# Moving operands 128 bytes further into their room: y's halves and the forms t1 and t3

## The chip, the cores and the metric

The kernel runs on one core of a Trainium2 chip. The metric is device time in microseconds (us) for one execution, taken as the median of the executions timed. The kernel before takes 1009.21 us, the median of three (1008.97, 1009.21 and 1009.24).

In the profile the engines are called PE (the matrix engine; PEld is its loading of stationary operands), DVE (the vector engine), ACT (the scalar engine), POOL and SP. ACT, DVE and POOL compute, and SP issues most of the transfers from device memory.

## The reference, cut to what matters

One block: a root-mean-square norm, one wide projection, two branches (a gated convolution and a state-space scan), a mixing product and a gated feed-forward. All of it is float32, with 512 tokens and a model width of 1024. The change touches an operand of two products: the gate-linear projection `u_glu` and the output product of the scan branch, `y @ out_w`.

```python
h = rms_norm(x, mix_pre_g[i])
proj = h @ w_in[i]
u_glu = proj[..., :OFF_Z]                 # val and gt of the gated convolution
...
val, gt = jnp.split(u_glu + glu_b, 2, axis=-1)
v = val * jax.nn.sigmoid(gt)
...
# scan branch
y = ssd_chunked(...)                      # [tokens, 2048]
y = y * jax.nn.silu(z)
yg = y.reshape(bsz, seqlen, N_GROUPS, D_INNER // N_GROUPS)
yg = yg * lax.rsqrt(jnp.mean(yg * yg, axis=-1, keepdims=True) + RMS_EPS)
y = yg.reshape(bsz, seqlen, D_INNER) * norm_g
ssm_out = y @ out_w                       # [512, 2048] @ [2048, 1024]
...
mixed = (g_conv * conv_out + g_ssm * ssm_out) @ w_out[i]
```

## The kernel before

**Split products.** PE multiplies in a rounded float32 format, so each float32 operand is kept as two halves, a high one and a low one, and each product is three matmuls into the same accumulator: high by high, high by low, low by high. `mm3` issues them (lines 426, 428 and 432). Each matmul has a stationary operand of 128 by 128, loaded first, and a moving operand that streams past it: 128 partitions by 512 columns (a whole row of tokens) or by 256 (half of it). In a row of the profile such as `pso<-yhl,whi` the accumulator stands before the arrow, then the moving operand, then the stationary one.

**The scan branch's output, `ssm_out`.** y comes in four pairs of groups, p = 0 to 3. For each pair the high and low halves of y lie in one tile, `yhl` (it is made again for every pair, always in the same room; its name in the trace drops the number). `s4` fills it: PE transposes y into an accumulator (`pyT`), ACT writes the high half (line 1051), DVE the low one (line 1052). `ssm_out` then makes 8 outputs `pso` per pair, each of 4 steps by 3 matmuls of 512 columns with `yhl` moving and the weights `whi` and `wlo` stationary: 4 x 8 x 4 x 3 = 384 matmuls. For p = 0, 1 and 2 they run in two runs of 48, for p = 3 in one of 96, broken in places by a few small matmuls of the scan.

**The gated projection's second half.** Units u = 0 to 3 use a scheme of seven half-size products in place of eight. Its moving operands are sums and differences of parts of h, each 256 columns wide: b11, b21 and b22 lie in `hhi` and `hlo`, and four forms t1 to t4 are made by `h_forms` (ACT on line 612 writes the high halves, DVE on line 613 the low ones). t1 and t3 share a tile in the room of `yhl` (which is free then), t4 and t2 a tile in the room called "so". The trace calls both tiles `h_t`. Each product is 4 steps by 3 matmuls. t2 is used in `glu_x` (stationary `whi_..S`, first half), t1 in `glu_v` (`whi_..s`, accumulator `pgv`), t3 in `glu_y` (`whi_..C`, accumulator `pgx`), b22 in `glu_w`, t4 in `glu_z`. So t1 and t3 move in 4 x 2 x 4 x 3 = 96 matmuls.

**Order.** The order of the instructions on every engine is written out in tables (`ORDER_ACT`, `ORDER_DVE`, `ORDER_PE`, and so on), which `in_written_order` enforces.

**Where the operands lie.** Tiles are laid out by pools with fixed places. In the built program the moving operands of these matmuls start, in bytes modulo 512, at the following places. Every step of an operand begins a multiple of 512 bytes after the last, so all steps share the place.

| moving operand | columns | place modulo 512 |
|---|---|---|
| `hhi`, `hlo` (whole rows: px, pB, pC, pgs, pgc) | 512 | 160 |
| `ehi`, `elo` (pg, pv in the first 40 us) | 512 | 160 |
| `yhl` (pso) | 512 | 32 |
| b11, b21, b22 in `hhi`, `hlo` (glu) | 256 | 160 |
| t1, t3 (glu) | 256 | 224 |
| t4, t2 (glu) | 256 | 352 |

The stationary operands of all these matmuls, `whi` and `wlo`, start at 160 modulo 512. `elo` lies in the same pool as `yhl`, `ehi` in the same room as t4 and t2. The room of `yhl` has 512 bytes more than y's halves fill, and the two offsets of the change (128 bytes, and 128 + 192) stay within them.

Of the kernel before, what the change touches and what calls it, by code (L numbers as in the profile page):

```python
# [11 lines left out]
F32R = mybir.dt.float32r  # L12
# [6 lines left out]
P = 128  # L19
T = 512  # L20
# [4 lines left out]
K2 = NK // 2  # L25
# [59 lines left out]
ADD_LO = (2, 3) + tuple(range(7, FF // P, 2))  # L85
GU_AHEAD = 5
MOV_AT = 192
S_AHEAD = 5

TAPS_GLU = 12  # L90
# [268 lines left out]
def block_kernel(ctx: ExitStack, tc: tile.TileContext, x, xT, x0, prm, hp, gp, wf, w, out):  # L359
# [87 lines left out]
    def col(name, i):  # L447
        o = PRM_OFF[name] + i
        return prm_t[:, o : o + 1]
# [25 lines left out]
    ssd = br.enter_context(tc.tile_pool(name="ssd", bufs=1))  # L475
# [12 lines left out]
    def aux_tile(name):  # L488
        return in_turn("aux", 2, 3, name)
# [107 lines left out]

    def h_forms():
        rooms = [p.tile([P, 8 * T + P], F32R, tag=tg, name=f"h_{n}") for p, tg, n in ((ssd, "yhl", "t13"), (sp, "so", "t42"))]
        both = [[r[:, MOV_AT // 4 + i * 4 * T : MOV_AT // 4 + (i + 1) * 4 * T].rearrange("p (n k t) -> p n k t", n=2, k=K2) for i in range(2)] for r in rooms]  # L600
        for f, two in zip(both, (("t1", "t3"), ("t4", "t2"))):
            for i, n in enumerate(two):
                HF[n] = [a[:, i] for a in f]
        for k in range(K2):
            (b11, b12), (b21, b22) = [(xk[q][:, :T2], xk[q][:, T2:T]) for q in (k, K2 + k)]
            dve.tensor_tensor(out=b11, in0=b11, in1=b12, op=ALU.subtract)
            dve.tensor_tensor(out=b12, in0=b22, in1=b12, op=ALU.subtract)
            dve.scalar_tensor_tensor(out=b22, in0=b22, scalar=-1.0, in1=b11, op0=ALU.mult, op1=ALU.subtract)
            dve.scalar_tensor_tensor(out=b21, in0=b22, scalar=-1.0, in1=b21, op0=ALU.mult, op1=ALU.subtract)
            for q, (hi, lo) in zip((k, K2 + k), both):  # L610
                t = xk[q].rearrange("p (n t) -> p n t", n=2)
                act.copy(hi[:, :, k], t)
                dve.tensor_tensor(out=lo[:, :, k], in0=t, in1=hi[:, :, k].bitcast(F32), op=ALU.subtract)
        for n, k0, c in (("b11", 0, slice(0, T2)), ("b21", K2, slice(0, T2)), ("b22", K2, slice(T2, T))):
            HF[n] = [a[:, k0 : k0 + K2, c] for a in (hhi, hlo)]
# [248 lines left out]
    proj_z0()  # L864
    time_steps()
    h_forms()
    for i, tg in enumerate(("xdt", "y")):
        n = seq["val", EARLY + 2] + i
# [171 lines left out]
    def s4(g):  # L1040
        s = st[g]
        yz = s["y"].rearrange("p c h d -> p c (h d)")
        if g % 2 == 0:
            yhl = ssd.tile([P, 8 * T + P], F32R, tag="yhl", name=f"yhl{g}")
            ys[g // 2] = [yhl[:, i * 4 * T : (i + 1) * 4 * T].rearrange("p (k t) -> p k t", k=4) for i in range(2)]
        yh, yl = ys[g // 2]
        for e in range(2):
            ps = aux_tile(f"pyT{g}_{e}")
            for c in range(NT):
                pe.transpose(ps[:, c * P : (c + 1) * P], yz[:, c, e * P : (e + 1) * P], ident)  # L1050
            act.activation(yh[:, 2 * (g % 2) + e, :], ps, AF.Copy, scale=col("norm_g", 2 * g + e))
            dve.scalar_tensor_tensor(
                out=yl[:, 2 * (g % 2) + e, :], in0=ps, scalar=col("norm_g", 2 * g + e),
                in1=yh[:, 2 * (g % 2) + e, :].bitcast(F32), op0=ALU.mult, op1=ALU.subtract,
            )
        del st[g]
# [18 lines left out]
    for g in range(G):  # L1075
# [5 lines left out]
        if g % 2 and g > 1:  # L1081
            s4(g - 2)
# [9 lines left out]
        if g % 2 == 0 and g > 1:  # L1092
            s4(g - 2)
# [35 lines left out]
    s1(G - 1)  # L1129
    gate("gs", 1, sg_tile("sgs1"))  # L1130
    s4(G - 2)
    s2(G - 1)
    gate("gs", 2, sg_tile("sgs2"))
# [12 lines left out]
    vp = mid.enter_context(tc.tile_pool(name="vT", bufs=1))  # L1146
    vp.tile([P, MOV_AT // 4], F32, name="vT_place")
    VF = {n: [vp.tile([P, K2, T2], F32R, name=f"v_{n}{p}") for p in "hl"] for n in ("t4", "b11", "b21", "t2", "t1", "t3", "b22")}
# [217 lines left out]
    mov, at = {}, [0]  # L1366

    def place_at(pool_, to):

        n = (to - at[0]) % 512  # L1370
        if n:
            pool_.tile([P, n // 4], F32, tag=f"place{at[0]}", name=f"place{at[0]}")
            at[0] += n

    place_at(h2p, MOV_AT)
    for n in MOV:
# [472 lines left out]
    for i, key in enumerate(STEPS):  # L1849
        while done_to < min(len(ahead), i + S_AHEAD + 1):  # L1850
            prep(ahead[done_to])
# [122 lines left out]
```

## Time and profile before

| what | value |
|---|---|
| median of the runs | 1009.21 us |
| the profiled execution's own time | 1009.96 us |
| its span, first to last instruction | 1008.2 us |
| granted PE clock over the span | 0.998 |
| PE busy | 1000.1 us (99%) |
| DVE busy | 875.3 us (87%) |
| ACT busy | 671.4 us (67%) |
| `pso` matmuls | 384 rows, 230 to 541 us |
| `pgv` and `pgx` matmuls with t1 or t3 | 96 rows, 70 to 101 us |

A row of a group of instructions gives line, engine, operation, tiles, shape and count, then after the bar the busy time in us, the mean duration of one in ns, and the idle time of the engine just before. Matmuls are pipelined: a 512-column matmul lasts some 390 ns from its start to its end, but the next one starts some 227 ns after it. What a matmul costs the engine is therefore read from the times at which rows start, in a view of the instructions in order of time, and not from its duration.

### The profile page before, as it was taken

What the parts mean: (1) busy time and instruction counts of PE and PEld (TensorE: products, weight loads), DVE (VectorE), ACT (ScalarE), POOL (GpSimd) and SP (SyncE); (2) the same over time, 40 slices, a digit from 0 to 9 for tenths busy, and PEclk for the clock granted to TensorE, in tenths of its full rate; (3) what the DMA queues carried; (4) which work ended last, traced back from release to release, by engine and by line L of the source; (5) the groups of instructions that cost most, each with busy time, mean ns of one, the idle gap of its engine ahead of it and who ended that gap; (6) DMA issues with size and microseconds to landing.
All of it is one profiled execution on the core that took longest, in us unless ns stands there. A gap on an engine that the chain in (4) does not pass through costs nothing.

```text
span 1008.2 us, 16310 instructions
## 1 busy us (share of the span) xinstructions
PE 1000.1 (99%) x6296; PEld 881.8 (87%) x6296; DVE 875.3 (87%) x1285; ACT 671.4 (67%) x1102; POOL 121.1 (12%) x145
## 2 busy tenths in 40 slices
PE   9999999999999999999999999999999999999997
PEld 7899889888888888888888889889999999998886
DVE  7899999838997999899996688889999897899974
ACT  8577789898667756854442585587666666667552
POOL 0210211110123022001110020011000000001001
PEclk9999999999999999999999999999999999999999
DMA  8755945646651684357453255646556455469622
GB/s 304 214 135 145 257 117 160 189 123 149 167 147 42 170 214 123 83 143 171 102 130 99 84 128 187 230 124 169 167 147 180 135 147 146 141 177 294 204 84 83
DMA packets 44557, 156.62 MB, mean 155 GB/s; under 512 B 5184, under 2 KB 6208, under 8 KB 43456
## 3 DMA queue, kind: packets, MB, share of 16 engines
q1 hardware_dynamic: 30672, 105.44, 31.3%
q0 software_dynamic: 11888, 44.57, 22.6%
q10 hardware_dynamic: 1920, 5.57, 1.6%
q8 instruction: 49, 0.80, 0.3%
q14 instruction: 28, 0.23, 0.1%
HBM read 151.31 MB, written 4.26 MB: 154 GB/s over the span
## 4 chain that ended last, share of the span: by engine, by line
PE 97%; DMA 1%; ACT 1%; DVE 0%; issue 0%; SPq 0%; POOL 0%; POOLq 0%; DVEq 0%; ACTq 0%
PE xy L432 4%; PE xy L426 4%; PE xy L428 4%; PE pso L426 3%; PE pz L428 3%; PE pz L432 3%; PE pz L426 3%; PE pso L432 3%; PE pso L428 3%; PE px L428 3%; PE px L426 3%; PE px L432 3%; PE yv L428 2%; PE yv L432 2%; PE yv L426 2%; PE yd L997 2%
## 5 line engine op out<-in xcount | busy, mean ns | idle before, releaser
L699 DVE SCALAR_TENSOR_TENSOR a<-v,prm_t,a 128x507 f32<-128x507 f32 (+20 forms) x240 | 171.5, 756 | 0.7
L391 ACT CAST whi<-raw 128x1024 fp32r<-128x1024 f32 x91 | 94.5, 1046 | 72.0 <-PE pso L428 27.4
L398 DVE TENSOR_TENSOR wlo<-raw,whi 128x1024 fp32r<-128x1024 f32 x54 | 65.6, 1218 | 32.2 <-ACT whi L391 32.2
L396 POOL DMA_DIRECT2D wlo<-in_w x37 | 32.9, 888 | 285.1 <-ACT wlo L395 83.4
L432 PE MATMUL pz<-whi,hlo 128*128 128x512 f32 (+2 forms) x160 | 56.1, 352 | 0.0
L428 PE MATMUL pz<-wlo,hhi 128*128 128x512 f32 (+2 forms) x160 | 55.8, 350 | 0.0
L426 PE MATMUL pz<-whi,hhi 128*128 128x512 f32 (+2 forms) x160 | 55.4, 352 | 0.0
L426 PE MATMUL pso<-yhl,whi 128*128 128x512 f32 x128 | 50.8, 399 | 0.0
L1407 ACT CAST whi_g<-raw 128x1024 fp32r<-128x1024 f32 x40 | 41.4, 1052 | 13.7 <-DVE raw L1438 7.5
L432 PE MATMUL pso<-yhl,wlo 128*128 128x512 f32 x128 | 50.4, 395 | 0.0
L426 PE MATMUL px<-hhi,whi 128*128 128x512 f32 x128 | 50.4, 393 | 0.0
L428 PE MATMUL pso<-yhl,whi 128*128 128x512 f32 x128 | 50.3, 395 | 0.0
L432 PE MATMUL px<-hhi,wlo 128*128 128x512 f32 x128 | 49.9, 389 | 0.0
L428 PE MATMUL px<-hlo,whi 128*128 128x512 f32 x128 | 49.8, 389 | 0.0
L1412 DVE TENSOR_TENSOR wlo_g<-raw,whi_g 128x1024 fp32r<-128x1024 f32 x34 | 41.2, 1220 | 3.4 <-ACT whi_g L1407 3.4
L682 ACT ACTIVATE L<-L,nacs 128x128 f32<-128x128 f32 x128 | 42.8, 392 | 1.3 <-POOL L L676 1.0
L890 DVE SCALAR_TENSOR_TENSOR x<-px,prm_t,x 128x511 f32<-128x511 f32 (+2 forms) x48 | 35.5, 743 | 6.2 <-ACT x L888 6.0
L395 ACT ACTIVATE wlo<-whi 128x1024 fp32r<-128x1024 f32 x37 | 39.1, 1058 | 0.4
L426 PEld LDWEIGHTS pz<-whi,hhi 128*128 128x128 f32 x160 | 30.2, 188 | 3.9
L428 PEld LDWEIGHTS pz<-wlo,hhi 128*128 128x128 f32 x160 | 30.2, 188 | 3.8
L432 PEld LDWEIGHTS pz<-whi,hlo 128*128 128x128 f32 x160 | 30.2, 188 | 3.8
L1407 ACT CAST chi_g<-raw 128x1024 fp32r<-128x1024 f32 x24 | 24.9, 1054 | 10.1 <-PE yv L428 3.4
(1046 smaller groups left out, 3618.1 us busy)
## 6 DMA issues: line engine op xcount, KB each, us to landing
raw<-in_w SPq DMA_DIRECT2D x182, 512.0 KB, 4.3
wlo<-in_w POOLq DMA_DIRECT2D x37, 512.0 KB, 5.8
L<-scr POOLq DMA_DIRECT2D x8, 1024.0 KB, 5.7
wlo_g<-in_w POOLq DMA_DIRECT2D x11, 512.0 KB, 5.8
sums<-in_w POOLq DMA_DIRECT2D x16, 256.0 KB, 4.5
clo_g<-in_w POOLq DMA_DIRECT2D x6, 512.0 KB, 5.7
pw_raws<-in_w SPq DMA_DIRECT2D x4, 512.0 KB, 6.2
xr<-in_x ACTq DMA_DIRECT2D x4, 512.0 KB, 4.2
```

The lines of the kernel that those rows point to most:

```text
L391: act.copy(hi[:, c], src)
L395: act.activation(lo[:, c], hi[:, c].bitcast(F32), AF.Copy, scale=-1.0)
L396: pool.dma_start(lo[:, c], w[n][:, c].bitcast(F32R), accum_op=ALU.add)
L398: dve.tensor_tensor(out=lo[:, c], in0=src, in1=hi[:, c].bitcast(F32), op=ALU.subtract)
L426: pe.matmul(ps, lh, rh, start=start, stop=False, skip_group_check=more)
L428: pe.matmul(ps, lh, rl, start=False, stop=False, skip_group_check=more)
L432: pe.matmul(ps, ll, rh, start=False, stop=stop, skip_group_check=more)
L682: act.activation(L[:, h, c, :], L[:, h, c, :], AF.Exp, bias=nacs[:, c, HG * g + h : HG * g + h + 1])
L699: return dve.scalar_tensor_tensor(out=va[j][:, d:], in0=vs[j][:, : T - d], scalar=col("dw_w", j * KC + KC - 1 - d), in1=va[j][:, d:], op0= ...
L890: dve.scalar_tensor_tensor(out=a[:, d:], in0=ps[:, : T - d], scalar=col("ssm_w", i * KS + KS - 1 - d), in1=a[:, d:], op0=ALU.mult, op1=ALU ...
L1407: act.copy(hi, src)
L1412: dve.tensor_tensor(out=lo, in0=src, in1=hi.bitcast(F32), op=ALU.subtract)
```

## The change

The tile `yhl` is viewed from 128 bytes into its room, so y's halves start at 160 modulo 512. The tile of t1 and t3, in the same room, is used from 128 + 192 bytes in, so these forms start at 352. The forms t4 and t2 stay where they are. No tile is moved or resized: every allocation of the built program has its address as before. The order of the instructions on all five engines is the same, row for row, and of the matmuls only the 384 with `yhl` and the 96 with t1 or t3 read from another address.

```diff
 MOV_AT = 192
+YHL_AT = 128
 S_AHEAD = 5
...
     def h_forms():
         rooms = [p.tile([P, 8 * T + P], F32R, tag=tg, name=f"h_{n}") for p, tg, n in ((ssd, "yhl", "t13"), (sp, "so", "t42"))]
-        both = [[r[:, MOV_AT // 4 + i * 4 * T : MOV_AT // 4 + (i + 1) * 4 * T].rearrange("p (n k t) -> p n k t", n=2, k=K2) for i in range(2)] for r in rooms]
+        both = []
+        for r, at in zip(rooms, (YHL_AT + MOV_AT, MOV_AT)):
+            r = r[:, at // 4 : at // 4 + 8 * T]
+            both.append([r[:, i * 4 * T : (i + 1) * 4 * T].rearrange("p (n k t) -> p n k t", n=2, k=K2) for i in range(2)])
...
         if g % 2 == 0:
-            yhl = ssd.tile([P, 8 * T + P], F32R, tag="yhl", name=f"yhl{g}")
+            yhl = ssd.tile([P, 8 * T + P], F32R, tag="yhl", name=f"yhl{g}")[:, YHL_AT // 4 :]
             ys[g // 2] = [yhl[:, i * 4 * T : (i + 1) * 4 * T].rearrange("p (k t) -> p k t", k=4) for i in range(2)]
```

## The prediction

> **What bounds the kernel now.** I read the page's busy times and its chain of waits first, then the list of who waited for whom on PE.
>
> ```profile
> PE 1000.1 (99%) x6296; PEld 881.8 (87%) x6296; DVE 875.3 (87%) x1285; ACT 671.4 (67%) x1102; POOL 121.1 (12%) x145
> PEclk9999999999999999999999999999999999999999
> PE 97%; DMA 1%; ACT 1%; DVE 0%; issue 0%; SPq 0%; POOL 0%; POOLq 0%; DVEq 0%; ACTq 0%
> ```
>
> ```profile
> engine line waited for: us in total, times, longest us
> PE warm_ps L510 <- DVE woken L505: 1.0, 1, 1.0
> PE pgx L432 <- DMA wlo_17A<-in_w: 0.4, 1, 0.4
> PE ptr L1504 <- ACT mg L1491: 0.2, 1, 0.2
> PE pv L746 <- DVE elo L544: 0.2, 1, 0.2
> ```
>
> PE is busy 99% of the span at full clock and makes 97% of the chain that ended last. It waits four times, 1.8 us in all: twice at the start, once for a transfer in the gated projection, and 0.2 us at a late transpose. So the time is the sum of the steps at which PE starts its matmuls, and a change is worth what it does to those steps, unless an input is then late.
>
> Next I compared the matmuls of 512 columns, grouped by tile and shape.
>
> ```profile
> L426 PE MATMUL pso<-yhl,whi 128*128 128x512 f32 x128 | 50.8, 399 | 0.0
> L432 PE MATMUL pso<-yhl,wlo 128*128 128x512 f32 x128 | 50.4, 395 | 0.0
> L426 PE MATMUL px<-hhi,whi 128*128 128x512 f32 x128 | 50.4, 393 | 0.0
> L428 PE MATMUL pso<-yhl,whi 128*128 128x512 f32 x128 | 50.3, 395 | 0.0
> L432 PE MATMUL px<-hhi,wlo 128*128 128x512 f32 x128 | 49.9, 389 | 0.0
> L428 PE MATMUL px<-hlo,whi 128*128 128x512 f32 x128 | 49.8, 389 | 0.0
> ...
> L428 PE MATMUL pg<-elo,whi 128*128 128x512 f32 x24 | 9.3, 389 | 0.0
> ```
>
> pso (moving at 32 modulo 512) lasts 6 ns longer than px and pg (moving at 160) on every line, with stationary operands at the same place. What counts is the step from start to start, so I took runs of these rows in order of time, from the first start to the start of the row behind the last.
>
> ```profile
> 257.20 0.40 PE L426 MATMUL pso<-yhl,whi 128*128 128x512 f32 x1
> ...
> 268.39 0.38 PE L1009 MATMUL pYa<-prev,C 128*128 128x256 f32 x1
> ...
> 528.19 0.39 PE L426 MATMUL pso<-yhl,whi 128*128 128x512 f32 x1
> ...
> 540.74 0.39 PE L426 MATMUL pgs<-hhi,whi 128*128 128x512 f32 x1
> ```
>
> ```profile
> 219.04 0.39 PE L426 MATMUL px<-hhi,whi 128*128 128x512 f32 x1
> ...
> 228.56 0.93 PE L1050 MATMUL pyT<-ident,y 128*128 128x128 f32 x7
> ...
> 282.91 0.39 PE L428 MATMUL pB<-hlo,whi 128*128 128x512 f32 x1
> ...
> 288.16 1.03 PE L985 MATMUL pSa<-xdec,BT 128*128 128x256 f32 x4
> ```
>
> 48 pso rows take 11.19 us (233.1 ns a step), and 54 of the last pair 12.55 us (232.4). 42 px rows take 9.52 us (226.7). 23 pB rows, a short run just after small matmuls and in the same stage as pso, take 5.25 us (228.3): its first steps are slow before it settles.
>
> **The change, part by part.** Nothing is added, removed or reordered, so there are three terms, two of PE steps and one of a wait.
>
> *pso.* 288 rows at 233.1 and 96 at 232.4 make a mean of 232.9 ns. At 160 the rows should step as other rows at 160 do: 226.7 if they settle as px does, 228.3 if every run is like pB's. pB's extra is (228.3 - 226.7) x 23 = 37 ns per start of a run; over a run of 48 that is 0.8 ns a row, so 227.5 with it and 226.7 without. I take the middle, 227.1, a gain of 5.8 ns a row: 384 x 5.8 = **2.23 us**. The ends are 384 x 4.6 = 1.77 (pB's pace) and 384 x 6.2 = 2.38 (px's).
>
> *t1 and t3.* At 256 columns the same comparison stands within unit 0, where t2 (352), t1 and t3 (224) and b22 (160) follow each other.
>
> ```profile
> 69.15 0.29 PE L426 MATMUL pgx<-h_t,whi_11S 128*128 128x256 f32 x1
> ...
> 69.51 0.28 PE L426 MATMUL pgx<-h_t,whi_11S 128*128 128x256 f32 x1
> ...
> 70.53 0.28 PE L426 MATMUL pgv<-h_t,whi_11s 128*128 128x256 f32 x1
> ...
> 73.36 0.28 PE L426 MATMUL pgv<-hhi,whi_11S 128*128 128x256 f32 x1
> ...
> 74.79 0.29 PE L426 MATMUL pgx<-h_t,whi_11C 128*128 128x256 f32 x1
> ```
>
> t1 and t3 take 2.83 us for 24 rows (117.9 ns). t2 takes 1.02 us for its last 9 (113.3), or 1.38 for all 12 (115.0) with the first three, which come from rows at another place. b22 takes 1.43 for 12 (119.2). After the change t1 follows t2 and t3 follows t1 at one place, so I take nearly the settled pace, a gain of 4.5 ns: 96 x 4.5 = **0.43 us**; ends 96 x 2.9 = 0.28 and 96 x 4.6 = 0.44.
>
> *The transfer that PE already waits for.*
>
> ```profile
> 78.84 0.87 POOL L810 DMA_DIRECT2D wlo_17A<-in_w  x1 [8.46 <-ACT wlo_17A L809]
> ```
>
> ```profile
> 80.41 0.28 PE L426 MATMUL pgv<-h_t,whi_11s 128*128 128x256 f32 x1
> ...
> 83.24 0.28 PE L426 MATMUL pgv<-hhi,whi_13S 128*128 128x256 f32 x1
> ...
> 86.82 0.39 PE L432 MATMUL pgx<-hhi,wlo_17A 128*128 128x256 f32 x1 [0.38 <-DMA wlo_17A<-in_w]
> ```
>
> The 24 rows of unit 1 (80.41 to 83.24) lie between the issue of that transfer at 78.84 and the end of PE's wait at 86.82. What they save PE only waits longer: 24 x 4.5 = **0.11 us** lost. Unit 0's 24 rows end before the issue, which follows ACT's work on PE's outputs and should come earlier with them; if it does not, 0.22 is lost, and if the issue were early enough nothing.
>
> *The writes.* ACT and DVE write y's halves and the forms at the new places too.
>
> ```profile
> L612 ACT CAST h_t<-xT x7: 600/616/621, 51.6 to 57.0; 128x512 fp32r<-128x512 f32 x7
> L613 DVE TENSOR_TENSOR h_t<-xT,h_t x7: 678/687/694, 52.2 to 65.7; 128x512 fp32r<-128x512 f32 x7
> ```
>
> On both engines these 7 writes go to both rooms, at 224 and at 352, and they last the same within 21 ns. So at most 21 ns on each of 20 writes per engine (16 of y, 4 of t1 and t3) could change: 0.4 us, spread over some 470 us in which PE waits for neither engine. I cost it at nothing; without that cover, 0.4.
>
> Sum: 2.23 + 0.43 - 0.11 = **2.55 us**, with ends 1.77 + 0.28 - 48 x 2.9 ns = 1.91 and 2.38 + 0.44 = 2.82. The profiled execution's own 1009.96 (span 1008.2 and 1.8 around it) would become 1007.4; it stands 0.75 above the median 1009.21, so I forecast a median of **1006.7 us** (1006.4 to 1007.3).
>
> [...]
>
> **The rivals.**
>
> *Nothing comes of it: the slower step belongs to the room or to what runs beside, not to the place.* yhl, t1 and t3 share one room, and all three step slowly. In the last stage some rows are slow although they move at 160:
>
> ```profile
> L428 PE MATMUL tm_d<-clo_g,f_Q 128*128 128x512 f32 x12 | 4.7, 394 | 0.0
> ```
>
> Their stationary operand lies elsewhere, though, and pso's does not. Against it also: `elo`, in the same pool, is at 389, and in the glu rows, side by side in the same 6 us, three places give three steps, the slowest (b22) in no shared room. The time would be 1009.2. [...]
>
> *PE gains, DVE does not follow.* While pso runs DVE is nearly full.
>
> ```profile
> 334.00:374.00 40.00, 40.00 (x234) 32.61 (x233) 39.86 (x58) 26.86 (x42) 6.00 (x6) 1.00 0.66 172
> ```
>
> DVE (third pair) is busy 39.86 of 40 us here. If PE ran into a wait for it in the first three pairs, their gain would go, and the last pair (96 x 5.8 = 0.56) and t1, t3 (0.32) would stay: 1009.21 - 0.88 = 1008.3. Against it: PE waits for DVE nowhere after the start, and DVE's lead shows before the mean over the channels, where all its convolution work must be done and DVE idles:
>
> ```profile
> 547.31 1.23 DVE L398 TENSOR_TENSOR wlo<-raw,whi 128x1024 fp32r<-128x1024 f32 x1 [4.29 <-ACT whi L391]
> ...
> 552.75 1.22 DVE L398 TENSOR_TENSOR wlo<-raw,whi 128x1024 fp32r<-128x1024 f32 x1 [3.61 <-ACT whi L391]
> ...
> 558.37 1.29 DVE L1164 SCALAR_TENSOR_TENSOR a<-plm,a 128x512 f32<-128x512 f32 x2 [3.80 <-PE plm L1160]
> ```
>
> 11.7 us of idle there is more than four times the gain.
>
> *Slower: moving and stationary operand at one place get in each other's way.* At 160 y's halves start at the same place as `whi` and `wlo`, which are loaded while the rows before stream.
>
> ```profile
> L428 PE MATMUL pso<-yhl,whi x128: 387/393/404, 237.3 to 540.3; 128*128 128x512 f32 x128
> ```
>
> If each row then went at the longest seen (404, against a mean of 396.3 over the three lines), that would be 384 x 7.7 = 2.96 us: 1012.2. It decides once pso's step passes 232.9. Against it: px pairs 160 with 160 and steps at 226.7.
>
> **How the numbers follow.** The forecast has a chance of 0.79, "nothing" 0.09, "DVE" 0.07, "slower" 0.05. 0.2% of the time is 2.02 us, about what a measurement of this kernel tells from no change. Of the forecast's 0.79, most lies above 2.02 and 0.03 between 1.91 and 2.02; of "slower", 0.01 is within 0.2%, and 0.01 of "DVE" passes it. So faster 0.76 + 0.01 = 0.77, same 0.03 + 0.09 + 0.06 + 0.01 = 0.19, slower 0.04. The likeliest's ends are 1006.4 to 1007.3; the runs shown spread by 0.3, and towards the DVE rival I go to 1007.9, so the range is 1006.2 to 1007.9.
>
> **What would show it.** In the changed kernel's profile the three pso rows should fall from 399, 395, 395 to about 393, 389, 389, a pso run of 48 from 11.19 to about 10.9 us, and the 24 rows of t1 and t3 in unit 0 from 2.83 to about 2.73. The wait for wlo_17A should grow from 0.4 to about 0.5, and PE's list of waits should gain no row. A pso step still near 233 means the place was not the cause; pso at 227 with a new PE wait after 230 us means the gain was given back; a step above 233 means the two operands collide.

## The result, and the profile after

The changed kernel takes 1006.97 us (median of 12 runs, 1006.03 to 1007.62), beside 1009.17 us for the kernel before on the same chip (12 runs, 1008.58 to 1009.97). The medians lie 2.2 us apart; the ratio is 0.9977, with a 95% interval of 0.9968 to 0.9986, so the change makes the kernel 0.23% faster. The span of the profiled execution went from 1008.2 to 1005.6 us.

The changed kernel's page, its row of busy times and the clock that PE was granted:

```profile
PE 997.9 (99%) x6296; PEld 882.1 (88%) x6296; DVE 876.2 (87%) x1285; ACT 670.9 (67%) x1102; POOL 122.1 (12%) x145
PEclk9999999999999999999999999999999999999999
```

PE's busy time fell by 2.2 us with the same 6296 matmuls and the same clock (0.998 before, 0.999 after), and the other engines are where they were. The groups of matmuls by shape (lines 426 to 432 of the kernel before are 427 to 433 here, and lines behind `h_forms` stand four lower) show which ones:

```profile
L427 PE MATMUL px<-hhi,whi 128*128 128x512 f32 x128 | 50.4, 394 | 0.0
L427 PE MATMUL pso<-yhl,whi 128*128 128x512 f32 x128 | 50.1, 394 | 0.0
L433 PE MATMUL px<-hhi,wlo 128*128 128x512 f32 x128 | 49.9, 390 | 0.0
L429 PE MATMUL px<-hlo,whi 128*128 128x512 f32 x128 | 49.8, 389 | 0.0
L433 PE MATMUL pso<-yhl,wlo 128*128 128x512 f32 x128 | 49.7, 390 | 0.0
L429 PE MATMUL pso<-yhl,whi 128*128 128x512 f32 x128 | 49.7, 389 | 0.0
```

The three pso rows went from 399, 395, 395 to 394, 389, 390 ns and now stand level with px. In order of time, the same stretches as were read of the kernel before:

```profile
70.95 0.28 PE L427 MATMUL pgv<-h_t,whi_11s 128*128 128x256 f32 x1
...
73.67 0.28 PE L427 MATMUL pgv<-hhi,whi_11S 128*128 128x256 f32 x1
...
236.75 0.39 PE L427 MATMUL pso<-yhl,whi 128*128 128x512 f32 x1
...
256.67 0.39 PE L427 MATMUL pso<-yhl,whi 128*128 128x512 f32 x1
...
267.55 1.02 PE L1013 MATMUL pYa<-prev,C 128*128 128x256 f32 x4
...
526.03 0.39 PE L427 MATMUL pso<-yhl,whi 128*128 128x512 f32 x1
...
538.27 0.39 PE L427 MATMUL pgs<-hhi,whi 128*128 128x512 f32 x1
```

The run of 48 pso rows takes 10.88 us (226.7 ns a step) where it took 11.19, the 54 of the last pair 12.24 (226.7) where they took 12.55, and the 24 rows of t1 and t3 in unit 0 take 2.72 us (113.3) where they took 2.83.

In the kernel before, the first pso row starts at 237.03:

```profile
237.03 0.40 PE L426 MATMUL pso<-yhl,whi 128*128 128x512 f32 x1
```

So the changed kernel is 0.28 us ahead there, and 540.74 - 538.27 = 2.47 us ahead at the first pgs row behind the last pso: the stretch that holds all 384 pso rows gave 2.19 us. The 0.28 before it is a loss and a gain together: PE reaches the first row of t1 0.42 us later than before (70.95 against 70.53), and from there to 236.75 it gains 0.70 us. The later start does not come from the change. It arises in the first rows of the program, whose operands have not moved, and it varies: in the seven profiles of kernels that differ from the kernel before only in t1, t3, y or later operands, the first row of t1 comes between 0.23 us earlier and 0.69 us later than there. PE's first row of pv lasts 0.47 us in the kernel before and 0.77 in the changed one:

```profile
4.37 0.47 PE L743 MATMUL pv<-ehi,whi 128*128 128x512 f32 x1
```

```profile
4.47 0.77 PE L747 MATMUL pv<-ehi,whi 128*128 128x512 f32 x1
```

Of the 0.70 us, 4 x 0.11 = 0.44 are the rows of t1 and t3, and 0.22 are a wait that became shorter:

```profile
79.14 0.87 POOL L814 DMA_DIRECT2D wlo_17A<-in_w  x1 [8.18 <-ACT wlo_17A L813]
```

```profile
86.78 0.39 PE L433 MATMUL pgx<-hhi,wlo_17A 128*128 128x256 f32 x1 [0.16 <-DMA wlo_17A<-in_w]
```

PE now waits 0.16 us for this transfer instead of 0.38. The transfer was issued 0.30 us later than before and PE still went on 0.04 us earlier. The list of waits on PE has no new row:

```profile
PE warm_ps L511 <- DVE woken L506: 1.0, 1, 1.0
PE ptr L1508 <- ACT mg L1495: 0.2, 1, 0.2
PE pgx L433 <- DMA wlo_17A<-in_w: 0.2, 1, 0.2
```

### The profile page after: what moved, and what is told of

Its sections match the earlier page's. It is cut to its first block, busy times and chain, and to the rows that moved or that the text cites. A ratio compares the mean times of both kernels' runs of the same rounds, so it can differ in the third digit from the quotient of the medians.

```text
span 1005.6 us, 16310 instructions
## 1 busy us (share of the span) xinstructions
PE 997.9 (99%) x6296; PEld 882.1 (88%) x6296; DVE 876.2 (87%) x1285; ACT 670.9 (67%) x1102; POOL 122.1 (12%) x145
## 4 chain that ended last, share of the span: by engine, by line
PE 97%; DMA 1%; ACT 1%; issue 0%; DVE 0%; POOL 0%; POOLq 0%; DVEq 0%; ACTq 0%
PE xy L427 4%; PE xy L433 4%; PE xy L429 4%; PE pz L429 3%; PE pz L433 3%; PE pz L427 3%; PE pso L427 3%; PE px L433 3%; PE pso L429 3%; PE pso L433 3%; PE px L427 3%; PE px L429 3%; PE yv L427 2%; PE yv L429 2%; PE yv L433 2%; PE yd L1001 2%
```

## The experiments

Two questions were open: whether each part of the change gives what it was costed at, and why the place matters at all. For the second, two theories were set against each other in the later runs. By the *place theory*, which is the prediction's, a matmul is slow because its moving operand starts at a bad place. By the *pair theory*, what counts is the distance between the places at which the moving and the stationary operand start.

### Each part alone

```diff
 # e1: y at 160; t1 and t3 back at 224
-        for r, at in zip(rooms, (YHL_AT + MOV_AT, MOV_AT)):
+        for r, at in zip(rooms, (MOV_AT, MOV_AT)):
```

> y's halves at 160, t1 and t3 back at 224. Place theory (the step of a matmul depends on where its moving operand starts modulo 512 bytes): pso steps at 227 ns, the t1 and t3 rows at 118 as before; the kernel is 384 x 5.9 = 2.3 us faster than before, about 1006.9, and its wait for wlo_17A is not changed by it. Room theory (the room or what runs beside is slow): pso stays at 233, no gain. A third reading, that the change's gain is mostly a shift of the wait for the transfer: under 1 us here.

```diff
 # e2: t1 and t3 at 352; y back at 32
-            yhl = ssd.tile([P, 8 * T + P], F32R, tag="yhl", name=f"yhl{g}")[:, YHL_AT // 4 :]
+            yhl = ssd.tile([P, 8 * T + P], F32R, tag="yhl", name=f"yhl{g}")
```

> t1 and t3 at 352, y's halves back at 32. Place theory: t1 and t3 rows step at 113.3 ns, pso at 233; 96 x 4.5 = 0.43 us less PE time, of which 0.1 to 0.2 may go into the wait for wlo_17A, so 0.2 to 0.4 us faster than before, too little to be told from no change. Room theory: 118 ns and no gain.

Each ratio from here on is to runs of the kernel before that were taken beside the run (medians of 1009.74 us here, 1009.52 and 1009.62 further down). y alone: 1007.33 us, 0.9977 of before (0.9968 to 0.9986). t1 and t3 alone: 1008.85 us, 0.9992 (0.9983 to 1.0001). With y alone the run of 48 pso rows takes 10.88 us and unit 0's 24 rows stay at 2.83:

```profile
70.96 0.28 PE L427 MATMUL pgv<-h_t,whi_11s 128*128 128x256 f32 x1
...
73.79 0.28 PE L427 MATMUL pgv<-hhi,whi_11S 128*128 128x256 f32 x1
...
256.75 0.39 PE L427 MATMUL pso<-yhl,whi 128*128 128x512 f32 x1
...
267.63 0.59 PE L1013 MATMUL pYa<-prev,C 128*128 128x256 f32 x2
```

With t1 and t3 alone the two are 11.19 and 2.72 us. So each part acts as if the other were not there, y is most of the gain, and what t1 and t3 give (0.44 us by their rows) is too little for the timed runs to tell from nothing. "Room or neighbours, not the place" falls: room, neighbours and order are the same in all four kernels.

### Other places for y

y's halves are written once for each of four pairs of groups, so one kernel tries four places.

```diff
 # e3: places 352, 96, 224, 288 for pairs 0 to 3
 # e4: (384, 448, 480, 512), places 416, 480, 0, 32
 # e5: (96, 112, 144, 160), places 128, 144, 176, 192;
 #     and rooms zip (288, 224): t1/t3 at 320, t4/t2 at 384
+YHL_ATS = (320, 64, 192, 256)
...
-            yhl = ssd.tile([P, 8 * T + P], F32R, tag="yhl", name=f"yhl{g}")[:, YHL_AT // 4 :]
+            yhl = ssd.tile([P, 8 * T + P], F32R, tag="yhl", name=f"yhl{g}")[:, YHL_ATS[g // 2] // 4 :]
```

> y's halves of the four pairs at four places in the same room: 352, 96, 224 and 288 modulo 512; t1 and t3 at 352. Read from the steps of pso in each pair. Place theory: four different steps, each the same in all runs of its pair; none need be 227, and 160 may or may not be the best. Room theory: all four at one step, 227 or 233. If the step only depends on whether the place is 32 modulo 128, all four are 227 to 233 alike (all four are 32 modulo 64).

> y's halves of the four pairs at 416, 480, 0 and 32 modulo 512; the last is 512 bytes further than in the kernel before, at the same place modulo 512. Place theory modulo 512: the last pair steps at 232.4 as before, though every address in it has moved by 512 bytes; the others at steps of their own. If the period is longer than 512 bytes, or the room's start counts, the last pair steps otherwise.

> y's halves of the four pairs at 128, 144, 176 and 192 modulo 512, 16 bytes and 32 bytes on each side of 160; t1 and t3 at 320, t4 and t2 at 384. If the step depends on the place modulo 256 (32 and 288 both gave 232.4, 160 and 416 both 227.2), none of these has been seen yet: the step may change within 16 bytes, or hold at 227 from 128 to 192. [...] A place below 226 would be a better one for y.

One run of each: 1008.23, 1007.91 and 1010.32 us. What counts in them is not the total but the step at each place. The first and last rows of runs of 48 pso steps, first with y at 352 and then at 224 (pairs 0 and 2 of e3):

```profile
256.24 0.39 PE L428 MATMUL pso<-yhl,whi 128*128 128x512 f32 x1
...
267.44 0.81 PE L1014 MATMUL pYa<-prev,C 128*128 128x256 f32 x3
...
463.84 0.40 PE L428 MATMUL pso<-yhl,whi 128*128 128x512 f32 x1
...
474.84 0.59 PE L1014 MATMUL pYa<-prev,C 128*128 128x256 f32 x2
```

11.20 us (233.3 ns a step) at 352 and 11.00 (229.2) at 224. The same with y at 416 and at 0 (pairs 0 and 2 of e4):

```profile
256.16 0.39 PE L428 MATMUL pso<-yhl,whi 128*128 128x512 f32 x1
...
267.04 1.02 PE L1014 MATMUL pYa<-prev,C 128*128 128x256 f32 x4
...
463.33 0.40 PE L428 MATMUL pso<-yhl,whi 128*128 128x512 f32 x1
...
474.55 0.59 PE L1014 MATMUL pYa<-prev,C 128*128 128x256 f32 x2
```

10.88 us (226.7) at 416 and 11.22 (233.8) at 0. 416 is 160 + 256, so the pattern repeats every 256 bytes and not only every 512: 480 (11.01 us, 229.4) goes with 224 in the same way, and 288 (12.55 us for the 54 rows of the last pair, 232.4) with 32. And with y at 176, 16 bytes beside the good place (pair 2 of e5):

```profile
465.77 0.39 PE L428 MATMUL pso<-yhl,whi 128*128 128x512 f32 x1
...
476.89 0.59 PE L1014 MATMUL pYa<-prev,C 128*128 128x256 f32 x2
```

11.12 us, 231.7 ns: three quarters of the gain is gone 16 bytes to one side, and all of it on the other (144: 11.20 us, 233.3). Of the nine places modulo 256 that were tried, a single one is good, and it is just where the stationary halves `whi` and `wlo` start. By the pair theory that is no accident.

### Everything behind the weights' pool moved, then the weights moved

```diff
 # e6: whi, wlo, hhi and hlo stay; y, ehi, elo, chi, clo at 32,
 #     t1..t4 and the feed-forward's forms at 224
-    place.tile([P, 40], F32, name="place")
+    place.tile([P, 8], F32, name="place")
```

> Everything behind the weights' pool lies 128 bytes earlier: y's halves are back at 32 and t1 and t3 at 224 as in the kernel before, and in other rooms ehi and elo go from 160 to 32, the seven forms of the feed-forward and of the pointwise product, and t4 and t2, from 352 to 224; hhi, hlo and the weights stay. Place theory: ehi and elo rows go from 227 to 232.5 ns (192 rows, 1.0 us), the 256-column rows from 113.6 to 117.8 (some 2,500 rows, 10 us), pso back to 232.9 (2.2 us): about 1020 us, clearly slower. Room theory: only pso, t1 and t3 change, about 1009.

1013.98 us, 1.0042 of before (1.0026 to 1.0059). pg, whose `ehi` and `elo` now start at 32, became long, as both theories have it:

```profile
L427 PE MATMUL pg<-ehi,whi 128*128 128x512 f32 x24 | 9.5, 398 | 0.0
L429 PE MATMUL pg<-elo,whi 128*128 128x512 f32 x24 | 9.5, 394 | 0.0
L427 PE MATMUL xy<-t2h,whi_g 128*128 128x256 f32 x56 | 15.5, 276 | 0.0
```

The total is well below what the place theory expected, mainly because the feed-forward's gate and up rows (xy, 256 columns, moving operand from 352 to 224) did not lengthen: 276 ns here, with the `whi_g` they meet still at 160, and 277 in the changed kernel. In steps from start to start, the 702 rows of xy that meet weights at 160 take 114.3 ns on average where they took 114.0. So 256 columns in that stage do not care about this place, although t1 and t3 do (117.9 ns at 224, 113.3 at 352), and so do the rows of the pointwise product (pwx, from 115.6 to 118.3 ns).

```diff
 # e7: whi and wlo at 288, everything else as in the changed kernel
+    wp.tile([P, 32], F32, name="wts_place")
...
-    place.tile([P, 40], F32, name="place")
+    place.tile([P, 8], F32, name="place")
```

> The weights whi and wlo at 288 instead of 160; everything else as in the changed kernel. They are the stationary operand of px, pB, pC, pgs, pgc, pso (moving at 160) and the moving one of pz and of the mixing product. Place theory: pso and px stay at 227 although their stationary operand has moved, and pz (moving at 288, the same as 32 modulo 256) goes from 227 to 232.4. Pair theory (what counts is the distance between moving and stationary): px and pso, now 128 bytes apart, go to 232 or so, and the kernel is slower by more than 1,500 x 5 ns = 8 us.

1019.82 us, one run. Here no moving operand of px, pg and pso starts anywhere new, and all of them became long (the rows of px and pso; the slowest of pg's groups of 24 went from 393 to 398 ns):

```profile
L428 PE MATMUL px<-hhi,whi 128*128 128x512 f32 x128 | 51.0, 399 | 0.0
L428 PE MATMUL pso<-yhl,whi 128*128 128x512 f32 x128 | 50.8, 399 | 0.0
L434 PE MATMUL pso<-yhl,wlo 128*128 128x512 f32 x128 | 50.3, 395 | 0.0
```

y stands at 160, where it was fast, and its first run of 48 rows takes 11.20 us again. The place theory falls with this run: 160 was not good beside weights at 288.

### The other operand, and the bad places made good

```diff
 # e8: hhi and hlo at 288, weights and y at 160
-    hp_pool.tile([P, 80], F32, name="hT_place")
+    hp_pool.tile([P, 48], F32, name="hT_place")
```

> hhi and hlo, in another room and pool, at 288 instead of 160; everything else as in the changed kernel. Place theory: the 1,152 rows of 512 columns with hhi or hlo moving go from 227.3 to 232.4 ns, 5.9 us slower than the changed kernel, about 1012.9; the 144 rows of 256 columns (b11, b21, b22) leave 160, their slow place, and may gain up to 6 ns each, 0.9 us. Room theory: no change, 1007.

1014.5 us, 1.0052 (1.0037 to 1.0067). px, whose moving halves went to 288, is long, and pso, untouched, is short. pz has the roles turned round: `whi` moves from 160 and `hhi`, `hlo` are stationary.

```profile
L427 PE MATMUL px<-hhi,whi 128*128 128x512 f32 x128 | 51.0, 399 | 0.0
L427 PE MATMUL pso<-yhl,whi 128*128 128x512 f32 x128 | 50.1, 394 | 0.0
L433 PE MATMUL pz<-whi,hlo 128*128 128x512 f32 x96 | 37.9, 397 | 0.0
```

The same row of pz in the changed kernel:

```profile
L433 PE MATMUL pz<-whi,hlo 128*128 128x512 f32 x96 | 37.4, 392 | 0.0
```

pz lasted 392 ns there and in the kernel before, and 397 here. Only its stationary operand was moved, so by the place theory it would have stayed; its 288 rows of 512 columns at 5 ns make 1.4 of the 1.6 us by which the total passes that theory's 1012.9.

```diff
 # e9: e7, with y at 32 and t1/t3 at 224 again (weights at 288)
-YHL_AT = 128
+YHL_AT = 0
```

> The halves of y stand at 32 modulo 512 again and t1/t3 at 224, where the kernel before had them, while all weight halves stand at 288 as in the run with the weights moved. Pair theory (a step of 512 columns is short where moving and stationary start at the same place modulo 256 bytes): y at 32 against weights at 288 is a distance of 0 modulo 256, so the 384 pso rows fall from the 232.2 to 233.3 ns of the run with y at 160 and the weights at 288 to about 227 ns; px, pB and pC (160 against 288) stay at 232.5; t1/t3 (224 against 288, the same distance as 352 against 160) come to 113.3 ns, or to a mix up to 118. The whole: 1019.8 - 384 x 5.7 ns = 1017.6 us, 1017.2 with the shorter t1/t3. Place theory (a row is long because its moving operand stands at a bad place of its own): y at 32 costs 232.9 ns as in the kernel before, and the whole stays at 1019.8 us or above.

1018.13 us, one run. This is the test that the two theories answer in opposite ways, and y at 32, the slow place of the kernel before, is fast beside weights at 288:

```profile
L428 PE MATMUL px<-hhi,whi 128*128 128x512 f32 x128 | 51.0, 399 | 0.0
L428 PE MATMUL pso<-yhl,whi 128*128 128x512 f32 x128 | 50.2, 394 | 0.0
L434 PE MATMUL pso<-yhl,wlo 128*128 128x512 f32 x128 | 49.7, 390 | 0.0
```

```profile
260.85 0.39 PE L428 MATMUL pso<-yhl,whi 128*128 128x512 f32 x1
...
271.75 1.03 PE L1014 MATMUL pYa<-prev,C 128*128 128x256 f32 x4
```

48 rows in 10.90 us, 227.1 ns a step. The total came 0.5 to 0.9 us above what was expected. One part of that is t1 and t3, which got their short step in units 1 and 2 (2.73 us for 24 rows) but not in units 0 and 3 (2.82), though their distance is the same in all four and the same as in the changed kernel; the rest is within what single runs of one kernel differ by (1006.03 to 1007.62 for the changed one).

With d the start of the moving operand less the start of the stationary one, modulo 256 bytes, the runs of pso rows go into one table. Each step is the length of one run (48 rows, or 54 in the last pair) over its count; where two stand for one pair of places, the first is from a run of 48 and the second from the 54.

| d | moving / stationary place, and the step in ns |
|---|---|
| 0 | 160/160: 226.7; 416/160: 226.7; 32/288: 227.1 |
| 16 | 176/160: 231.7 |
| 32 | 192/160: 233.3 |
| 64 | 224/160: 229.2; 480/160: 229.4 |
| 96 | 0/160: 233.8 |
| 128 | 32/160: 233.1 and 232.4; 288/160: 232.4; 160/288: 233.3 and 232.4 |
| 192 | 352/160: 233.3; 96/160: 233.3 |
| 224 | 128/160: 233.3 |
| 240 | 144/160: 233.3 |

### The pair rule put to use

The down projection (tm) moves weights from 160 past the activations' halves, which are stationary; those in the six shared rooms start at 352, a distance of 64. 64 bytes further on they are at a distance of 0. Each of these rooms grows by 256 bytes, so in the built program about half of the halves come to 416 and the others to 160, and some moving forms of the gate and up products go from 352 to 96: more than the expectation below says, but 256 bytes change no distance modulo 256.

```diff
+F_AT = 64
...
-        mov[n] = [h2p.tile([P, KB, HB], F32R, tag=f"m_{n}{p}", name=f"{n}{p}") for p in "hl"]
+        mov[n] = []
+        for p in "hl":
+            more = F_AT // 4 if f"{n}{p}" in ROOMS else 0
+            room = h2p.tile([P, KB * HB + 4 * more], F32R, tag=f"m_{n}{p}", name=f"{n}{p}")
+            mov[n].append(room[:, : KB * HB].rearrange("p (k t) -> p k t", k=KB))
...
-        t = slot(r, [P, 2, 2, HB], f"f_{name}", F32R)
+        at = F_AT // 4
+        t = slot(r, [P, 4 * HB + 4 * at], f"f_{name}", F32R)[:, at : at + 4 * HB]
+        t = t.rearrange("p (a b t) -> p a b t", a=2, b=2)
```

> Everything as in the changed kernel, but the halves of the feed-forward's activations that are stationary in the six shared rooms stand 64 bytes further, at 416 modulo 512 in place of 352. Their 347 product rows of 512 columns move the down projection's weights, which start at 160: the distance modulo 256 goes from 64 to 0, and nothing else moves. Pair theory: these rows fall from 228.9 to about 227.0 ns, 347 x 1.9 ns = 0.66 us, and the whole to about 1006.3 us, 0.7 us under the changed kernel. Rival, that the place of the stationary operand does not matter at a distance that is small already, or that the stage ends by other work than TensorE's: the rows or the whole stay, 1007.0 us.

> The changed kernel itself, on the same chip and beside the same runs of the kernel before as the run with the feed-forward's stationary halves moved: 1007.0 us, 0.9977 of the kernel before, with its 347 product rows at 228.9 ns.

1005.91 us (5 runs), 0.9964 of before (0.9951 to 0.9978), beside 1007.17 us (11 runs) and 0.9977 (0.9968 to 0.9985) for the changed kernel in the same comparison; the profiled spans are 1004.5 and 1005.2 us. The rows at issue, first in the changed kernel and then with the halves moved: one line of a group, and the first row of a run of 72 with the row behind its last.

```profile
L429 PE MATMUL tm_d<-clo_g,f_Q 128*128 128x512 f32 x12 | 4.7, 394 | 0.0
```

```profile
897.28 0.39 PE L427 MATMUL tm_c<-whi_g,f_T 128*128 128x512 f32 x1
...
913.76 0.39 PE L427 MATMUL tm_c<-whi_g,fh_T 128*128 128x512 f32 x1
```

```profile
L430 PE MATMUL tm_d<-clo_g,f_Q 128*128 128x512 f32 x12 | 4.7, 389 | 0.0
```

```profile
897.39 0.39 PE L428 MATMUL tm_c<-whi_g,f_T 128*128 128x512 f32 x1
...
913.71 0.39 PE L428 MATMUL tm_c<-whi_g,fh_T 128*128 128x512 f32 x1
```

The 72 rows take 16.32 us (226.7 ns a step) where they took 16.48 (228.9). Over all 347 rows the step falls from 228.9 to 226.7 ns, 0.78 us. The 0.7 us between the two spans is about that, and about the 0.66 expected; the 1.3 us between the medians is more than the rows explain, and the two intervals overlap. It is the fastest kernel of this study, by its median and by its rows.

## Why the prediction was right, and where it was not

The predicted 1006.7 us and its range of 1006.2 to 1007.9 hold the measured 1006.97, and the two larger terms have their size. The reason given for them was only half of the truth. The number did not depend on it: px, from which pso's new pace was taken, pairs 160 with 160, just as pso does after the change, and t2 pairs 352 with 160, as t1 and t3 then do. So the comparison was sound under either theory. In part the close hit is luck: by their rows the two terms gave 2.19 + 0.44 = 2.63 us, and a later start of 0.42 us and a wait shorter by 0.22, neither of them forecast, moved the profile by amounts that change from run to run.

- *pso, 2.23 us.* The stretch from the first pso row to the first row behind the last one became 2.19 us shorter. Settled runs went all the way to px's 226.7 ns. The whole stretch gave 5.7 ns a row (2.19 us over 384) and not 6.2, because the first rows behind other work gained little, as pB's short run had suggested: in the run that starts at 452.13 us in the changed kernel, the second to the tenth row step at 231 ns, against 233 in the kernel before.
- *t1 and t3, 0.43 us.* Unit 0 became 0.11 us shorter, 4 x 0.11 = 0.44 in all, the settled pace that was taken.
- *The wait for wlo_17A.* The sign was wrong. A loss of 0.11 us was expected, with the wait growing to 0.5; it shrank to 0.16. This wait varies from profile to profile by more than the term: with y alone moved, with t1 and t3 alone moved, and in a second profile of the changed kernel it has no row in the list at all. From the issue of the transfer to the start of PE's row that waits for it, 7.98 us passed in the kernel before and 7.64 in the changed one, so the transfer's own time moved the wait by more than the rows did. A single trace's 0.38 us was taken for a property of the kernel.
- *The writes.* As costed, nothing: the 16 writes of y by ACT and by DVE last as long as before (medians of 683 and 744 ns, against 684 and 745):

```profile
L1055 ACT ACTIVATE yhl<-pyT,prm_t x16: 670/683/702, 186.5 to 517.0; 128x512 fp32r<-128x512 f32 x16
L1056 DVE SCALAR_TENSOR_TENSOR yhl<-pyT,prm_t,yhl x16: 740/744/752, 189.0 to 517.8; 128x512 fp32r<-128x512 f32 x16
```

- *DVE does not follow.* No wait for DVE appeared; PE kept the gain of the first three pairs, and DVE's idle time before the mean over the channels is still 11.7 us.
- *Nothing: room or neighbours.* It fell with y alone moved, within one room: the run of 48 pso rows stepped at 226.7 ns there, against 233.1 in the kernel before.
- *Slower: moving and stationary operand at one place.* The prediction thought that two operands at one place might get in each other's way, and gave that 0.05. It is the other way round: of the distances tried, equal places modulo 256 bytes are the one fast case (226.7 to 227.9 ns a step over a run of pso). The rival had the right two operands and the wrong sign.

The step that failed is the first sentence of the pso term, "at 160 the rows should step as other rows at 160 do". It held because everything at 160 in this kernel meets weights at 160. What the runs showed in its place is that the distance to the stationary operand modulo 256 decides: y at 160 stepped at 233.3 ns beside weights at 288, and y at 32 at 227.1. The prediction had the row that says so: `tm_d<-clo_g,f_Q`, slow although its moving operand is at 160, was set aside with "their stationary operand lies elsewhere", which was the answer.

The faster by 0.23% that was measured lies just past the 0.2% named as telling, and its interval (0.14 to 0.32%) reaches below it; the rows, more than the median, are what tie the gain to the change.

**What stays open.** Why the distance matters was not tried. The runs with the weights or y moved show that it does matter for 512 columns (y at 160 steps at 226.7 ns beside weights at 160 and at 233.3 beside weights at 288); but whether the reads of the two operands meet, or something else goes with the addresses, no run here tells. Nor do the runs tell whether a row's own stationary operand counts or the next row's, which is loaded while the row streams (in the changed kernel the pso row at 256.67 lasts 0.39 us, and the load for the row that starts at 256.89 runs from 256.67 for 0.19): in the stretches measured both start at the same place, and the six or seven borders of each sort in the down projection do not settle it. For 256 columns the rule is not the same and not settled. There equal starts are not the fast case: b22, at d = 0, steps at 119.2 ns in the kernel before. t1 and t3 are fast at d = 192 (2.72 us for 24 rows in every unit of the changed kernel, 2.83 at d = 64 in the kernel before), yet at the same two places they took 2.83 us in units 0 to 2 and 2.72 in unit 3 when only `hhi` and `hlo` had moved. So these rows have two paces at one and the same distance, and the gate and up rows keep one pace at two distances (114.0 ns at 192, 114.3 at 64). What runs just before may carry over; that was not isolated, and the gain of t1 and t3 is therefore measured but not explained.

## What to carry to other kernels

Where PE is the bound and each matmul loads its own weights, compare the step from start to start of rows of one shape, and write beside each the start of *both* operands: a difference of a few ns between rows of one shape is worth the count of the rows. Of the distances tried here, only equal starts modulo 256 bytes gave the 512-column step of 226.7 ns, and that held whichever of the two operands was moved to match the other. Moving an operand that many others are matched to can cost far more than it gives: with the weights at 288 the kernel took 1019.82 us. For rows of 256 columns nothing of this may be assumed. A row in the trace that the favoured explanation has to excuse is worth an experiment before the forecast is settled.

## What the runs showed of the hardware

- In the runs of 48 and 54 pso rows, a 512-column matmul with a new stationary operand each time steps at 226.7 to 227.9 ns when both operands start at the same place modulo 256 bytes, at 229.2 to 229.4 with the moving one 64 bytes on (228.9 in the down projection), and at 231.7 to 233.8 at the other distances tried.
- The good place is narrow: 16 bytes to either side cost 5.0 and 6.6 ns.
- The sign counts: d = 64 is better than its mirror image d = 192 (229.2 against 233.3).
- It holds with the roles turned round: with the stationary activations 128 bytes off, pz's matmuls went from lasting 392 ns to 397, and with those of the down projection moved from 64 to 0 its step went from 228.9 to 226.7.
- 256-column rows react otherwise: t1 and t3 step at 113.3 or 117.9 ns at one and the same distance (192), b22 at 119.2 with equal starts, and the feed-forward's gate and up rows at 114.0 and 114.3 at distances of 192 and 64.
